# Channel shuffle in place through PSUM: from twenty tiles of 8 to 32 KB in six buffers to twelve tiles of 40 KB and one of 32 in five

## The chip, the cores and the metric

The kernel runs on one core of one Trainium2 chip. The metric is the device time of one execution in microseconds (us). HBM is the chip's main memory; SBUF, with 128 partitions, and PSUM are memories of the core. KB is 1024 bytes here, and MB in rates is a million bytes.

## The reference, cut to what matters

The input is 16 x 64 x 64 positions of 256 float32 channels: 67.11 MB in, 67.11 MB out. Within each position the channels are read as 8 groups of 32 and written transposed.

```
x = x.reshape(batch, h, w, groups, channels_per_group)
x = x.transpose(0, 1, 2, 4, 3)
x = x.reshape(batch, h, w, c)
```

Nothing is computed. The work is to move 134.2 MB through the core, with a permutation of 256 floats on the way.

## The kernel before

A tile of size `q` is `128 * q` positions. Each of the 128 partitions holds `q` positions of 1 KB each, which also lie together in HBM. That piece of `q` KB in one partition is called a *row* below. SyncE issues the load. VectorE permutes 8 positions at a time from the buffer into PSUM, ScalarE copies them back into the same buffer, and ScalarE's queue issues the store.

```
_SIZES = [8] + [32] * 14 + [24, 8, 8, 8, 8]
_BUFS = 6
_PIECE = 8
...
    biggest = max(_SIZES)
    ...
    first = 0
    for q in _SIZES:
        buf = pool.tile([P, biggest * c], F32, name="buf")
        nc.sync.dma_start(out=buf[:, : q * c], in_=rows(x_flat, first, q))
        for k in range(0, q, _PIECE):
            piece = buf[:, k * c : (k + _PIECE) * c]
            bounce = psum.tile([P, _PIECE * c], F32, name="bounce")
            nc.vector.tensor_copy(
                out=bounce.rearrange("p (i j g) -> p i j g", j=CPG, g=G),
                in_=piece.rearrange("p (i g j) -> p i j g", g=G, j=CPG),
            )
            nc.scalar.copy(out=piece, in_=bounce)
        nc.scalar.dma_start(out=rows(out_flat, first, q), in_=buf[:, : q * c])
        first += P * q
```

## Time and profile before

| | before |
|---|---|
| time, median of 3 runs | 320.13 us (319.8 to 320.82) |
| span of the profiled run | 317.8 us |
| VectorE busy | 228.2 us, 72% |
| ScalarE busy | 120.7 us, 38% |
| DMA rate, 60 to 260 us | 434 GB/s |

From the profile page of the kernel before come the engines' busy time, the DMA row (tenths of the 16 DMA engines' time in 40 slices), the two queues (packets, MB, share of the 16 engines' span), and VectorE's group of copies:

```profile
DVE 228.2 (72%) x64; ACT 120.7 (38%) x65; POOL 0.2 (0%) x4
...
DMA  8999999999999999999999999999999999999995
...
q1 hardware_dynamic: 2880, 67.11, 49.4%
q10 hardware_dynamic: 2880, 67.11, 49.0%
...
L54 DVE COPY bounce<-buf 128x2048 f32<-128x2048 f32 x64 | 228.2, 3633 | 83.0 <-DMA buf<-in_x_dram 83.0
```

The DMA engines are full from the second slice to the last but one. In the packet records only queue q1 moves data in the first 10 us, when nothing is stored yet, so q1 carries the loads and q10 the stores. As engine time, 49.4% of 317.8 us is 157.0 us of loads, and 49.0% is 155.7 us of stores. Every wait of VectorE ends at a load.

The chain of waits of the kernel before (start us, length us, what) shows the rhythm:

```profile
176.15 14.26 DVE bounce L54 x4
190.41 5.00 another core or an unknown queue
...
195.50 14.26 DVE bounce L54 x4
```

The line "another core or an unknown queue" is the view's name for a wait that it cannot place; here VectorE waits for a load, since all its idle time ends at one. A tile of 32 KB becomes ready every 19.35 us, and VectorE needs 14.26 us of that. Two transfers of 4.19 MB in 19.35 us make 433 GB/s, so the tile period is the time the DMA engines need.

The trace also holds a record of each packet, with queue, start, duration and size. One row is one packet. A row of 32 KB takes 1213 ns on one of the 16 engines, load or store, and a row of 8 KB takes 309 ns (medians; the first loads take longer). Each engine carries 8 of a transfer's 128 rows.

### The profile page before, as it was taken

The numbers are of one execution on the slowest core, as the hardware profiler recorded it, in microseconds if no ns is written. First come the engines' busy times: TensorE is split into PE (matmuls) and PEld (weight loads), VectorE is DVE, ScalarE is ACT, GpSimd is POOL, SyncE is SP. The second block draws the span as 40 slices with busy tenths as digits, with TensorE's granted clock in tenths as the row PEclk, the third lists the DMA queues.
The fourth block names the chain that finished last, engine by engine and source line by source line (L and its number), as shares of the span: only waits on it lengthen the run. The fifth ranks groups of instructions, "written<-read, shape, count | busy, mean of one in ns | idle before, by whom it ended". The sixth has DMA issues, their size and how long they took to land.

```text
span 317.8 us, 277 instructions
## 1 busy us (share of the span) xinstructions
DVE 228.2 (72%) x64; ACT 120.7 (38%) x65; POOL 0.2 (0%) x4
## 2 busy tenths in 40 slices
DVE  3199999893975939679395893939849497980471
ACT  1225545453351524424244252542505345242222
POOL 0000000000000000000000000000000000000000
DMA  8999999999999999999999999999999999999995
GB/s 330 406 434 413 429 429 449 408 458 417 445 429 429 445 412 458 400 462 425 433 434 425 449 408 454 429 437 429 429 446 412 442 443 438 418 417 439 413 403 215
DMA packets 5762, 134.24 MB, mean 422 GB/s; under 512 B 640, under 2 KB 640, under 8 KB 640
## 3 DMA queue, kind: packets, MB, share of 16 engines
q1 hardware_dynamic: 2880, 67.11, 49.4%
q10 hardware_dynamic: 2880, 67.11, 49.0%
q14 instruction: 2, 0.02, 0.0%
HBM read 67.11 MB, written 67.11 MB: 422 GB/s over the span
## 4 chain that ended last, share of the span: by engine, by line
DVE 59%; DMA 23%; another core or an unknown queue 15%; issue 1%; ACT 1%; SPq 0%; DVEq 0%
DVE bounce L54 59%; DMA buf<-in_x_dram 13%; DMA out_dram<-buf 9%; ACT buf L58 1%; SPq L50 0%; DVEq L54 0%
## 5 line engine op out<-in xcount | busy, mean ns | idle before, releaser
L54 DVE COPY bounce<-buf 128x2048 f32<-128x2048 f32 x64 | 228.2, 3633 | 83.0 <-DMA buf<-in_x_dram 83.0
L58 ACT COPY buf<-bounce 128x2048 f32<-128x2048 f32 x64 | 119.4, 1865 | 186.9 <-DVE bounce L54 186.9
L58 ACT ACT_TABLE_LOAD x1 | 1.3, 1283 | 5.6 <-DMA buf<-in_x_dram 5.6
L77 POOL MEMSET const-bfloat16-1.0<- 128x1 bf16 x1 | 0.1, 102 | 0.0
L77 POOL MEMSET const-uint8-127<- 128x1 uint8 x1 | 0.1, 101 | 0.0
L77 POOL MEMSET const-float32-0.0<- 128x1 f32 x1 | 0.1, 99 | 0.2 <-issue 0.2
L77 POOL MEMSET const-float32-1.0<- 128x1 f32 x1 | 0.1, 98 | 0.0
## 6 DMA issues: line engine op xcount, KB each, us to landing
buf<-in_x_dram SPq DMA_DIRECT2D x14, 4096.0 KB, 61.9
out_dram<-buf ACTq DMA_DIRECT2D x14, 4096.0 KB, 35.7
buf<-in_x_dram SPq DMA_DIRECT2D x5, 1024.0 KB, 35.2
out_dram<-buf ACTq DMA_DIRECT2D x5, 1024.0 KB, 9.9
buf<-in_x_dram SPq DMA_DIRECT2D x1, 3072.0 KB, 59.2
out_dram<-buf ACTq DMA_DIRECT2D x1, 3072.0 KB, 18.8
```

Of the source, the lines that this page charges most:

```text
L54: nc.vector.tensor_copy(out=bounce.rearrange("p (i j g) -> p i j g", j=CPG, g=G), in_=piece.rearrange("p (i g j) -> p i j g", g=G, j=CPG),)
L58: nc.scalar.copy(out=piece, in_=bounce)
L77: nc = _bacc.Bacc("TRN2", target_bir_lowering=False, num_devices=1)
```

## The change: its intent, and the diff

The intent is fewer and larger transfers. There are 13 loads and 13 stores instead of 20 and 20, in 200 KB of buffers a partition instead of 192. The small tiles at the start and the end go.

```
-_SIZES = [8] + [32] * 14 + [24, 8, 8, 8, 8]
-_BUFS = 6
+_SIZES = [40] * 12 + [32]
+_BUFS = 5
```

## The prediction

> **What bounds the kernel now.** The transfers. The page's DMA row reads 9 tenths or more in every slice but the first and the last two; the two queues together hold the 16 DMA engines 98% of the span (section 3: 49.4% and 49.0%). VectorE is busy 72%, ScalarE 38%, and VectorE's 83.0 us of idle time all end at a load (the waits). In the packet records of the trace a row of 32 KB takes 1213 ns on one engine and a row of 8 KB 309 ns, for loads and stores alike: 16 engines make 432 and 424 GB/s. The Trainium skill, page "DMA: Bandwidth & Descriptors", section "Where 436 GB/s comes from", gives a ceiling of 435 GB/s; this trace agrees. The chain of waits names VectorE for 59%, but its pieces only fill the time between load landings 19.4 us apart, which is what 8.4 MB take at 432 GB/s.
>
> **Costs, as engine time.** Each engine carries 8 rows of every transfer. Before: 16 x (14 x 1213 + 912 + 5 x 309) = 311.0 us. The first packet effectively begins at 2.3 us and the last ends at 316.7, so the engines stand idle 3.4 us: 0.4 and 2.4 us are seen in the packet records before the last two stores of 1 MB (at 308.7 and 311.7), where the end waits for the last small loads, one VectorE piece (3.6) and one ScalarE piece (1.9); the rest is a slow start. After: a 40 KB row should take about 1514 ns (estimate, from 309 and 1213), so 16 x (12 x 1514 + 1213) = 310.1 us: 0.9 us fewer, from fewer rows.
>
> **The start.** The first tile lands at about 16.2 us (the same 5.2 MB land there now) instead of 5.5; its five pieces take 17.8 us, so the first store leaves at 36 instead of 11. This costs nothing: five loads (26 MB, 61 us) are queued and keep the engines full.
>
> **The middle.** The queues share by turns, row by row: stores of 32 KB rows get 341 GB/s against 80 for loads of 8 KB rows around 270 us. The skill's section "Queues, rings and completion order" says the same (round-robin by packet). With equal rows a load lands every 24.2 us; VectorE needs 17.8. A buffer comes free about 27 us before its load's turn.
>
> **The end.** The last load lands near 280 us (range 277 to 285). Then 4 x 3.57 + 1.9 + about 1.3 us of issue put the last store's first packet near 298. Until about 303 the engines still have stores 10 and 11 to write, so the 16 us of copying are hidden, with some 5 us to spare. The last 30 us are stores alone; then 9.7 us of last store. The two late bubbles (2.8 us) go.
>
> **Sum.** 317.8 - 0.9 - 2.8 = 314.1 us span, so 320.13 - 3.7 = 316.4; I add 0.2 for stores running alone (late 8 KB packets take up to 335 ns against 309). Predicted 316.6 us, 315.0 to 319.4. Faster by over 2% 0.04, within 2% 0.93, slower 0.03.
>
> **What would show it.** First store issued at 36 us; loads landing 24.2 us apart; about 1514 ns per 40 KB packet; last load at 277 to 285 us; no idle DMA slice before the last; last store issued before the previous store lands; VectorE still 228 us.
>
> **What would make it wrong.** The last load landing after 285 us, or stores held by a wait for another transfer, would expose the last tile's copying, up to some us. Stores alone at 5% less rate would add 1.6 us. Rows over 32 KB might be cut or run slower. If the bubbles now are made good elsewhere, the gain is 1 us.

## The result, and the profile after

| | before | after |
|---|---|---|
| time, median of 5 runs | 320.13 us (319.67 to 320.82) | 352.72 us (352.52 to 353.81) |
| span of the profiled run | 317.8 us | 351.3 us |
| DMA rate, 60 to 260 us | 434 GB/s | 397 GB/s |
| period of a tile | 19.35 us per 32 KB | 28.1 us per 40 KB |

The changed kernel is 10% slower: the ratio is 1.1023, with a 95% interval of 1.1001 to 1.1045. A ratio here is the mean time of one kernel's fast runs over that of the other's from the same rounds, so it is not quite the ratio of the medians.

The same lines of the page, now of the changed kernel:

```profile
DVE 227.7 (65%) x64; ACT 120.7 (34%) x65; POOL 0.2 (0%) x4
...
DMA  8999999999999999999999999999999999889290
...
q10 hardware_dynamic: 1872, 67.11, 50.0%
q1 hardware_dynamic: 1872, 67.11, 44.7%
...
L54 DVE COPY bounce<-buf 128x2048 f32<-128x2048 f32 x64 | 227.7, 3633 | 103.2 <-DMA buf<-in_x_dram 103.2
```

The two queue lines hold the answer to "which side". Loads take 44.7% of 351.3 us, that is 157.0 us, exactly as before. Stores take 50.0%, that is 175.7 us: 20 us more for the same bytes. The DMA engines read as busy in the middle of the run. They are not idle; they are slow at storing.

The chain of waits of the changed kernel:

```profile
179.77 17.80 DVE bounce L54 x5
197.57 10.25 another core or an unknown queue
...
207.91 17.81 DVE bounce L54 x5
...
309.93 6.64 another core or an unknown queue
...
316.66 10.71 DVE bounce L54 x3
```

A tile becomes ready every 28.1 us, where 10.49 MB at 433 GB/s would need 24.2. The last tile is ready at 316.6 us instead of near 280.

The packet records show where the 28.1 us come from. While both queues run, the 40 KB load packets still take 1514 ns in the median, as expected. The store packets between 60 and 260 us have a mean of 1787 ns and a median of 1799, and they differ by engine. Where only loads run (after the first packets), they take 1514 ns; where only stores run at the end, 1515 to 1531.

**How the engines are told apart.** A packet record does not name its engine. But an engine does one packet after the other, so the records can be strung into 16 chains by letting each packet start where one of the 16 last ended. In the changed kernel 143 of 3744 records do not fit their chain within 40 ns by the stringing (a second one, which also requires 8 rows a transfer, left up to 192), and two engines that end a packet at the same instant can be swapped. I therefore rely on what a chain shows early in the run, up to 100 us.

Such a chain alternates strictly: one load packet, one store packet. The Trainium skill, page "DMA: Bandwidth & Descriptors", section "Queues, rings and completion order", says that each engine takes turns between queues at packet boundaries, and this trace agrees with one row per turn. In the changed kernel two chains ran their stores at about 2000 ns, most at about 1800, and two or three at 1514. The slowest need 1514 + 2000 ns for a load row and a store row, and 8 such pairs take 28.1 us. That is the tile's period. A transfer has landed only when its slowest engine is through (same page, section "Why a DMA increments its semaphore by 16 and not by 1"), so two slow engines set the pace for all.

A first suspect is cleared by the same trace. Of the 40 KB store packets between 60 and 260 us, the 279 during which VectorE was idle took 1804 ns on average, and the 599 during which it was busy throughout took 1782 ns. The 323 stores beside which ScalarE was idle took 1788 ns. The copying is not what slows the stores. This agrees with the skill's page "SBUF — State Buffer", section "Who interferes with whom", which says that a DMA never contends with a compute engine.

### The profile page after: what moved, and what is told of

Read it like the earlier page. It is cut to its first block, busy times and chain, and to the rows that moved or that the text cites. A ratio compares the mean times of both kernels' runs of the same rounds, so it can differ in the third digit from the quotient of the medians.

```text
span 351.3 us, 236 instructions
## 1 busy us (share of the span) xinstructions
DVE 227.7 (65%) x64; ACT 120.7 (34%) x65; POOL 0.2 (0%) x4
## 3 DMA queue, kind: packets, MB, share of 16 engines
q1 hardware_dynamic: 1872, 67.11, 44.7%
## 4 chain that ended last, share of the span: by engine, by line
DVE 62%; another core or an unknown queue 25%; DMA 4%; issue 2%; DVEq 1%; ACT 1%
DVE bounce L54 62%; DMA buf<-in_x_dram 4%; DVEq L91 1%; ACT buf L58 1%; DVEq L54 0%
## 5 line engine op out<-in xcount | busy, mean ns | idle before, releaser
L54 DVE COPY bounce<-buf 128x2048 f32<-128x2048 f32 x64 | 227.7, 3633 | 103.2 <-DMA buf<-in_x_dram 103.2
```

What stands on the lines that cost most here:

```text
L54: nc.vector.tensor_copy(out=bounce.rearrange("p (i j g) -> p i j g", j=CPG, g=G), in_=piece.rearrange("p (i g j) -> p i j g", g=G, j=CPG),)
```

## The experiments

The theories at the start were: **A**, a store packet over 32 KB is slow beside loads; **B**, rows 40 KB apart in HBM are slow; **C**, buffers 40 KB apart in SBUF are slow. Theory **D** came from the first four runs. Runs of the kernel before on the same chip took 319.8 to 320.4 us in the median each time. Where only one run was made, its state is unknown; differences of a per cent are not read from those.

### 1. Cutting the transfers, and other row sizes

Stores cut in two (the loads are cut in the same way in the second run):

```
-        nc.scalar.dma_start(out=rows(out_flat, first, q), in_=buf[:, : q * c])
+        half = q // 2 * c
+        for a, z in ((0, half), (half, q * c)):
+            nc.scalar.dma_start(
+                out=rows(out_flat, first, q)[:, a:z], in_=buf[:, a:z]
+            )
```

> The changed kernel with each store cut into two transfers of half a row (20 KB packets, same places in HBM and SBUF). Theory A (a store packet longer than 32 KB is slow beside loads): store packets near 760 ns, that is 27 B/ns, and 316 to 323 us. Theory B (rows 40 KB apart in HBM are what is slow) and theory C (buffers and rows of 40 KB in SBUF are): stores still some 15 to 30% above 757 ns, 340 us or more.

Measured: 321.6 us, store packets of 761 ns. Taken alone, this looks like theory A.

> The changed kernel with each load cut into two transfers of half a row; the stores keep 40 KB packets. Theory A: store packets stay near 1790 ns while loads run, 343 to 356 us; if it is the load's length that hurts the store beside it, stores fall to 1514 ns and 316 to 323 us. Theories B and C: 340 us or more.

Measured: 337.5 us, outside the ranges of all three theories. The store packets still had 40 KB, and most took 1514 ns; only late in the run did a few engines reach 1800 ns. A store of 40 KB beside a load is thus not slow as such, which speaks against A.

```
+_SIZES = [24] * 21 + [8]
+_BUFS = 8
```

> Twenty-one tiles of 24 KB and one of 8, eight buffers (192 KB). Theory A: 24 KB packets at 912 ns for both queues, 316 to 321 us. Theory B (a row pitch in HBM that is no power of two is slow): store packets well above 912 ns, 335 us or more. Theory C says nothing firm, buffers are 24 KB apart.

Measured: 317.7 us, all packets at 912 ns. A pitch in HBM that is no power of two is not slow as such.

```
+_SIZES = [32] * 16
+_BUFS = 5
-    biggest = max(_SIZES)
+    biggest = 40
```

> Sixteen tiles of 32 KB in five buffers that lie 40 KB apart in SBUF. Theories A and B: 1213 ns a packet for both queues as in the kernel before; about 320 us, a few more for the last tile of 32 KB. Theory C: store packets slow, 340 us or more.

Measured: 331.9 us, between the ranges of the theories. Rows of 32 KB, the size that had always taken 1213 ns, were now slow on some engines and not on others. This was the useful surprise, because the chains of one and the same run could be compared.

On five of the chains the first store packet came after 25 load packets, and on eleven after 26. Between 60 and 100 us the store packets of the five took 1397 ns on average, and those of the eleven 1221 ns. Each tile gives an engine 8 rows. After 25 loads the store of row 0 follows directly on the load of row 0 of the fourth tile, then row 1 follows row 1, and so on, since the queues take turns. After 26 loads the store of row 0 follows the load of row 1. Rows with the same number lie in the same partition. In the changed kernel 13 chains have the count 25 and 3 have 24; in the kernel before, the load next to a store lies 21 to 23 rows further on than that store in the middle of the run, on nearly all turns (in step it would be 24).

**Theory D**: a store becomes slow on an engine where it comes directly after the load of the same row number of a later tile. The moment at which the first store joins the queue decides this, and the taking of turns keeps it so.

Two checks from the traces belong here. In load_halves, after 100 us, the 157 stores that came directly after a load of the same row number took 1755 ns on average and 672 others took 1532. That speaks for D with load packets of half the length, but before 100 us 160 such stores took 1525 ns: equal row numbers alone are not enough. In store_halves only 33 stores, and in rows24 none, came directly after a load of their own row number, so these two fast runs hardly test D.

### 2. Moving one instruction

The first store is held back until the second tile's first piece has been copied; everything else is as in the changed kernel:

```
-    for q in _SIZES:
+    held = None
+    for tile_no, q in enumerate(_SIZES):
...
+            if held is not None and k == 0*_PIECE:
+                nc.scalar.dma_start(**held)
+                held = None
-        nc.scalar.dma_start(out=rows(out_flat, first, q), in_=buf[:, : q * c])
+        store = dict(out=rows(out_flat, first, q), in_=buf[:, : q * c])
+        if tile_no == 0:
+            held = store
+        else:
+            nc.scalar.dma_start(**store)
```

> The changed kernel; only the store of the first tile is issued after the first piece of the second tile instead of before it, 3.55 us later (one instruction moved on ScalarE). Theory D (a store is slow where, on its engine, it takes turns with the load of the same row number of a later tile; the row numbers lock when the first store joins the queue): the loads are then some 2 rows further on, all 40 KB store packets near 1514 ns, 315 to 320 us. Theories A (packets over 32 KB), B (rows 40 KB apart in HBM) and C (40 KB in SBUF): unchanged, 350 us or more.

Measured: 354.0 us (353.4 to 354.5 in 4 runs), ratio to before 1.1055 (1.1032 to 1.1078). By its time this is a miss for D. Its chains say the opposite (records between 60 and 100 us):

```
loads before the first store   engines   mean store packet
25                                   1             2181 ns
26                                  15             1514 ns
```

Fifteen engines were cured. One had loaded one row fewer when the store joined, fell into step, and held up every tile. The queue shares show it: the stores' mean cost fell, and the time did not. The lines are from the page of this run; 45.5% of 351.7 us is 160.0 us, against 175.7 in the changed kernel.

```profile
span 351.7 us, 237 instructions
...
q10 hardware_dynamic: 1872, 67.11, 45.5%
q1 hardware_dynamic: 1872, 67.11, 44.7%
```

The expectation also had the delay wrong. The first store left at 36.00 us in the changed kernel and at 37.39 here, 1.4 us later and not 3.55. ScalarE's queue issues a held store while the copy ahead of it still runs. So the store was moved again, behind the third piece (`k == 2*_PIECE`). It left at 44.61 us, 8.6 us later than in the changed kernel, and at 44.48 in the timed run below (the text says 10.6 us later):

> The changed kernel with the first store issued three pieces (10.6 us) later. In the run with one piece of delay, 15 engines began their first store after the second row of the fourth load and ran stores at 1514 ns; one engine began it after the first row (so load and store take turns on equal row numbers) and ran them at 2000 to 2400 ns, and every tile waited for it. Theory D: now all 16 begin some 3 to 5 rows later, no engine is slow, 315 to 321 us. If some engine or other is slow whatever the row numbers: 345 us or more.

Measured: 317.8 us, all engines at 30 or 31 rows, all stores at 1514 ns. The same file was timed at the end:

> The same file as later_first_store (317.8 us once), timed. Theory D, with the first store joining 30 or 31 rows of loads in, far from 25 or 33: 316 to 320 us in every run, that is, about 10% faster than the changed kernel and 0 to 1% faster than the kernel before. If the cure was luck: some runs above 330 us.

Measured: 317.46 us (317.1 to 317.77 in 5 runs), ratio to the kernel before 0.9922 (0.9908 to 0.9935). Tiles, row length, row pitch, buffers and copies are those of the changed kernel; only one store left later. This is the main result, and it refutes A, B and C as causes that would suffice by themselves. The timeline of the changed kernel and then of this one shows the first store's issue (start us, length us):

```profile
36.00 0.38 ACTq L59 DMA_DIRECT2D out_dram<-buf  x1
```

```profile
44.48 0.37 ACTq L61 DMA_DIRECT2D out_dram<-buf  x1
```

The queues, from the page of the timed run, have equal shares again:

```profile
span 315.3 us, 237 instructions
...
q1 hardware_dynamic: 1872, 67.11, 49.8%
q10 hardware_dynamic: 1872, 67.11, 49.2%
```

### 3. Putting a fast order of the tiles into step

If D is right, an order of tiles that is fast by itself must become slow when its first store is moved into step. The fast order has the tile of 32 KB first:

```
-_SIZES = [40] * 12 + [32]
+_SIZES = [32] + [40] * 12
```

> The same tiles with the one of 32 KB first instead of last, five buffers of 40 KB. The first store then joins at another row of the loads (estimate: after 22 or 23 rows instead of 25). Theory D: row numbers unequal, stores at 1514 ns, 315 to 321 us (the last tile is 8 KB larger). Theories A and B (length or HBM row pitch): 350 us or more.

Measured: 318.9 us, 22 or 23 rows loaded at the first store, all 40 KB stores at 1514 ns. Then its first store was held back by one piece, with the edit of experiment 2:

> The tiles of small_tile_first (318.9 us), with its first store held back by one piece (3.55 us), the same move that cured the other order. Theory D: the first store now joins after 24 or 25 rows of loads instead of 22 or 23; the engines with 25 take turns on equal rows, their stores go to 1750 ns or more, and the time to 335 to 356 us. If small_tile_first was fast for another reason (its small tile): 317 to 322 us.

Measured: 317.0 us. The move missed its mark. The store left at 30.90 instead of 29.42 us, for the reason given above, and joined after 23 rows on all 16 engines. It does not test D, except that 23 is fast. Held back by two pieces (`k == 1*_PIECE`):

> The tile of 32 KB first (317.0 and 318.9 us in two forms), its first store now held back by two pieces: in the trace of the form held by one it left at 30.9 us and joined after 23 rows of loads on every engine; 3.55 us or 2.3 rows later it should join after 25 rows on some or most engines and 26 on the rest. Theory D: the engines with 25 take turns on equal rows, stores of 1750 ns and more on them, 335 to 356 us. If this order of tiles is immune: 316 to 322 us.

Measured: 352.4 us (350.5 to 355.7 in 4 runs), ratio to before 1.1022 (1.0960 to 1.1083). From the chains, 60 to 100 us:

```
loads before the first store   engines   mean store packet
25                                   3             2205 ns
26                                  12             1514 ns
27                                   1             1514 ns
```

(The second stringing puts 13 engines at 26 and none at 27; the times are the same.)

A delay of 3.7 us on one instruction (the timelines have it at 30.90 and at 34.61 us) turned 317 into 352 us. The chains of waits show the period of a tile, first of the kernel held by one piece:

```profile
208.29 17.80 DVE bounce L55 x5
226.09 6.30 another core or an unknown queue
...
232.48 17.80 DVE bounce L55 x5
...
281.10 14.25 DVE bounce L55 x4
```

That is 24.2 us a tile, with the last load at 281 us, as the prediction had it. Then the same moments of the kernel held by two, in the windows view (DVE and ACT busy, POOL, clock, DMA share, GB/s):

```profile
60.00:260.00 200.00, 127.54 (x36) 68.49 (x37) 0.00 (x0) 1.00 0.99 414
260.00:300.00 40.00, 28.29 (x8) 13.06 (x7) 0.00 (x0) 1.00 0.86 356
300.00:360.00 60.00, 25.11 (x8) 14.93 (x8) 0.00 (x0) 1.00 0.48 207
```

Three engines of sixteen are late, and towards the end the other thirteen have nothing left to do until those have caught up: at 298, 306 and 330 us three packets are in flight.

### 4. HBM or SBUF?

Equal row numbers mean the same partition in SBUF and the same place within a tile in HBM. Two runs moved the HBM side alone. They give a wrong result: every load but the last reads `x` further on, by 20 KB in the first run and by one row, 40 KB, in the second.

```
-        nc.sync.dma_start(out=buf[:, : q * c], in_=rows(x_flat, first, q))
+        skip = 5120 if first + P * q < b * h * w else 0     # 10240 in the second
+        nc.sync.dma_start(
+            out=buf[:, : q * c],
+            in_=x_flat[first * c + skip : (first + P * q) * c + skip].rearrange(
+                "(p f) -> p f", p=P
+            ),
+        )
```

> Wrong result on purpose: the changed kernel, but every load except the last reads x 20 KB further on. Row numbers, partitions and turns stay as they are; only the distance in HBM between what a load reads and what the store beside it writes is no longer a whole number of MiB. Theory D1 (the clash is in HBM, by that distance): store packets fall towards 1514 ns, 315 to 325 us. Theory D2 (the clash is in SBUF, both in the same partition): store packets stay near 1790 ns, 345 us or more.

> Wrong result on purpose: the changed kernel, every load but the last reads x 40 KB (one row) further on. What lies in HBM beside a store is then what the fast engines of late_first_store had; the rows in SBUF and the turns stay equal. Theory D1 (HBM): 315 to 325 us. Theory D2 (SBUF or the engine's own turns): store packets near 1790 and 2000 ns, 345 us or more.

Measured: 352.8 and 352.4 us, and store packets as in the changed kernel (means of 1755 and 1761 ns from 60 to 260 us). The distance in HBM between what is read and what is written plays no part at these two shifts. In the second run the load read just what an engine out of step would have read.

The next run moved the buffers in SBUF apart by 1 KB (`biggest = 41`):

> The changed kernel with its five buffers 41 KB apart in SBUF instead of 40; rows, HBM and turns unchanged. If slow stores need equal rows and a certain distance in SBUF between the load's and the store's buffer (rows of 32 KB were slow 40 KB apart and fast 32 KB apart): stores faster than 1790 ns, below 340 us. If the distance plays no part: 350 us or more.

Measured: 352.9 us. The chains were clean here. Fourteen engines with 25 loads at the first store had mean store packets of 1764 to 2000 ns (60 to 100 us); two with 24, where the store comes just *before* the load of its row number, had 1514 ns. In load_shift40k the second stringing gives the two engines with 24 stores of 1514 ns too; in load_shift20k one of three with 24 had 1749, which swapped chains can explain, and nothing is built on it. In all these runs the slow engines had the one count of 25, so they do not tell equal row numbers from that count; the check on load_halves, with other counts, speaks for row numbers.

### 5. Rows of 32 KB in step: a weaker clash, and a false trail

> Sixteen tiles of 32 KB in five buffers, now 32 KB apart in SBUF. Theory C (the spacing of 40 KB): 318 to 323 us. Theory D: as with 40 KB spacing, that is, those engines slow whose first store joins after the load of the fourth tile's first row: 325 to 335 us.

Measured: 319.4 us, though 11 engines stood at 25. It looked as if buffers 32 KB apart were immune.

> Sixteen tiles of 32 KB in five buffers 40 KB apart as before, with the first store issued 3.55 us later. Theory D: all engines out of step by about 3 rows, all stores 1213 ns, 317 to 322 us. Theory C: 330 us as before.

Measured: 317.9 us, fifteen engines at 27 loads with 1213 ns, one at 26 with 1232 ns. The cure of experiment 2 also works for the 32 KB rows of rows32_apart40. Three timed runs then tested whether the spacing matters (`biggest` of 32, 40 and 36):

> The same file as rows32_five, timed: equal rows on most engines, buffers 32 KB apart. If 32 KB spacing makes equal rows harmless: 318 to 322 us in every run. If the first run was luck: some runs at 325 us or more.

> The same file as rows32_apart40, timed. If the spacing matters: 326 us or more in every run. If it is luck which engines join where: runs spread between 319 and 335 us as in rows32_five_again.

> Sixteen tiles of 32 KB in five buffers 36 KB apart. If any spacing that is not a multiple of 32 KB is open to the clash: 326 us or more, with stores above 1300 ns on engines of equal rows. If only the moment of joining counts: as rows32_five_again.

| buffers apart | runs, us | engines at 25: store packet | engines at 26 |
|---|---|---|---|
| 32 KB, first run | 319.4 | 11: 1221 ns | 5: 1218 ns |
| 32 KB, again | 318.7, 320.9, 321.7, 333.5 | 8: 1278 ns | 8: 1221 ns |
| 36 KB | 319.2, 319.2, 328.7, 328.8 | 11: 1236 ns | 5: 1220 ns |
| 40 KB, first run | 331.9 | 5: 1397 ns | 11: 1221 ns |
| 40 KB, again | 322.8, 323.5, 327.7, 337.6 | 7: 1281 ns | 9: 1222 ns |

(The packets are those of the profiled run of each, 60 to 100 us.) The immunity did not hold: in the second profile of the same file the stores in step took 1278 ns. The stores in step are longer in four of the five profiles, by a different amount each time; 1221 against 1218 in the first is no difference. On the engines at 26 it is the loads that are longer, 1223 to 1249 ns on average in the five profiles against 1213. A load and a store together take 2435 ns at 25 and 2440 at 26 in the first row of the table, and 2449 and 2451 with 36 KB; in the other three rows the engines at 25 take 34 to 169 ns more. So with 32 KB rows D accounts for part of what is seen, and why those loads are longer is open. One file spreads over 15 us. The runs 1.5% above the fastest count as slow and are left out (ratio 1.0006 for 32 KB apart and 1.0090 for 40 KB apart). That these runs are slow because of the clash is not shown, since no profile was taken of them. Whether the spacing has a small effect of its own stays open. It is not needed for the 10%, which experiment 2 removed with the spacing unchanged.

## Why the prediction was wrong

- **First store at 36 us instead of 11.** Right: 36.00 us.
- **A 40 KB packet takes about 1514 ns.** Right for loads once the run has started (median 1514 ns), for stores out of step (1514) and for stores alone (1515 to 1531). VectorE's 227.7 us are as predicted too.
- **"With equal rows a load lands every 24.2 us."** This is the step that failed. It took the 1514 ns to hold for stores in turn with loads, because the trace of before shows a median of 1213 ns for both, and in it the queues are never seen to run in step. In step, the stores of the slowest engines took 2000 ns, and a load landed every 28.1 us. The prediction had the turns (row by row) and the moment of the first store, and did not ask which rows would meet.
- **"The start costs nothing."** This failed for the same reason. A later first store costs no idle DMA time, but it decided in which step the two queues run for the next 250 us.
- **The last load near 280 us, with the copying hidden.** It landed at 316.6 us, outside the range. The delay is that of the middle: from there to the end it took 34.7 us (351.3 less 316.6), where the prediction had about 34 (314.1 less 280). The copying was not hidden, though: from 325 to 334 us the DMA engines were busy a share of 0.33 only.
- **The named risk "rows over 32 KB might be cut or run slower".** The direction was right, the reason wrong. Rows of 40 KB run at full rate when out of step (experiments 2 and 3), and rows of 32 KB can be slow in step (experiment 5).
- **The sum.** Where the clash is absent the rest of the calculation holds. The prediction was 316.6 us; the same 13 tiles out of step took 317.46 us (0.8% faster than before, timed) and 317.0 us (one run, tile of 32 KB first), with a tile period of 24.2 us and the last load at 281 us in the latter. In the kernel before the issue does not show, because its loads run 21 to 23 rows ahead and not 24. Whether its small first tile brings that about was not tested.

What stays open is the clash itself. With 40 KB stores the chains show it where row numbers are equal and the store comes directly after the load, though not in every such place (load_halves before 100 us). It sets in some rows after the queues have joined (after three or four rows in the changed kernel, about ten in rows32_apart40), and it costs 250 to 720 ns a 40 KB row (per-engine means from apart41 and small_first_held2 less 1514). HBM distance (at two shifts), the copying by VectorE and ScalarE, and row pitch by itself are excluded. Equal partition in SBUF remains, but no run separated "same partition" from another property of the engine's turns, so it is not shown.

## What to carry to other kernels

When two DMA queues are full, look at how they take turns as well as at the rate. Compare the queues' shares of the span for equal bytes: 44.7% against 50.0% here was the first sign that stores had become slow. A tile lands with the slowest of 16 engines, so a mean over engines hides the cause; compare the engines within one run. If loads and stores use tiles of equal size, choose the first tile or the moment of the first store so that they run out of step by several rows, and time the choice over several runs: one store moved by 8.5 us was worth 10%.

## What the Trainium skill lacked or had wrong

- Page "DMA: Bandwidth & Descriptors", section "Queues, rings and completion order": it describes the turns by packet, and the trace agrees, but it does not say that a store directly after the load of the same row number of another tile can be slow. Here that was 1764 to 2235 ns instead of 1514 for 40 KB (per-engine means in apart41 and small_first_held2), while loads stayed at 1514 to 1542 ns on average.
- The same page, section "Why a DMA increments its semaphore by 16 and not by 1": true, but the section gives no figure for what one slow engine costs. One engine of 16 at 2181 ns a store held a kernel at 354.0 us whose other fifteen ran their stores at 1514 ns.
- Page "DMA: Bandwidth & Descriptors", section "Rules for kernel authors", asks for 128 partitions and at least 1 MiB per DMA for the highest bandwidth. Every transfer of the changed kernel meets that, and from 60 to 260 us it ran at 397 GB/s; out of step the same transfers ran at 433 (timed run of later_first_store). The rule is not enough for two queues in turn.
- No page has a spread like that of the 32 KB rows in five buffers: 318.7 to 321.7 us in three runs of one file and 333.5 in a fourth, all at a granted clock of 1.00. The fourth counts as slow and was not profiled, so its cause is not shown.
